# A hybrid decoder layer: state-space products in plain float32, and another order of the projection's column blocks

## The chip, the cores and the metric

The kernel runs on one NeuronCore of a Trainium2 chip. Times are microseconds on the device for one execution of the whole program; the times shown are of separate runs, the profile of one more. PE is the matrix engine (TensorE) and PEld its weight loads, DVE the VectorE, ACT the ScalarE, POOL the GpSimd, and SP the SyncE, whose queue issues all the DMAs of this kernel.

## The reference

One inference step of one decoder layer, for a prompt of 1024 tokens and 8 x 4 sampled tokens, model width 1024, everything in float32:

```
proj = rmsnorm(h) @ w_in                    # 1024 x 3072: x_ssm | z_ssm | q | k | v | z_attn, 512 each
# state-space branch: 32 groups of 16 channels, each with one 64-dim complex diagonal state
bu   = u @ Bb                               # complex
x_t  = lam * x_{t-1} + bu_t                 # scan over time
y    = Re(C x) + D u
y    = glu(gelu(y)) * silu(z_ssm)
# attention branch: 8 heads of 64; softmax over keys at three (window, dilation) patterns,
#   (128,1), (512,4), (2048,16); times silu(z_attn); the sampled tokens also look into a key and value cache
out  = rmsnorm(h + concat(rmsnorm(y_ssm), rmsnorm(y_attn)) @ w_out)
```

The prompt's keys and values, the sampled tokens' new rows and the final states are outputs too.

## The kernel before

**Numbers in two parts.** PE takes two kinds of four-byte operands here: `float32` and a rounded form, `float32r`. Nearly all products of the kernel keep precision by hand: `split` (lines 137 to 143) makes of a tile a rounded part hi (ACT copies it into a `float32r` tile, line 139) and the rest lo (DVE subtracts hi from the tile, line 140), and a product becomes three `float32r` products, hi*hi, hi*lo and lo*hi, summed in PSUM. A few products work on `float32` tiles as they are: the taps (line 622), the column sums (lines 859, 861, 1605), the products with cached values (1361, 1373), and the transposes against the identity.

**Stages.** First the inputs are normalised, transposed and split. Then the projection runs by 12 blocks of 256 columns of `w_in`: `FIRST_BLOCKS` (8 and 0), the seven of `SSM_BLOCKS`, then 6, 10 and 11 in a later stage. A block's weights come in two DMAs and are split (`win`, lines 142 and 143; 12 buffers, 8 to a block). Blocks 0 to 7, 10 and 11 come out with columns on partitions, 144 products of 352 tokens each (line 314), into two PSUM banks (`mm`) in turn; what empties a bank depends on the block: for q and k (4 to 7) a split into `eq` tiles (lines 378, 379), for z_ssm (2, 3) a tanh and a product into `stp` (lines 341 to 344), for x_ssm (0, 1) a copy. Blocks 8 and 9, the values, come out with tokens on partitions, 192 products of 256 columns (line 294), emptied by a copy on ACT (line 305), and 16 more for the sampled rows (line 410).

**The state-space stage.** Beside these blocks, `ssm(o)` works on the 32 channel groups, four at a time (o = 0 to 7). 8 tokens make one step of the scan, so that a group has 128 steps and 8 sampled rows, W = 136 columns (144 with the rows of the sampled tokens' states). A call loads `u` from DRAM, builds on POOL and DVE the matrix that takes 8 x 16 inputs to a state (`wa`, transposed on PE), the one that takes a state to 8 x 16 outputs (`f`) and rotations `rc`, `rs`, makes the direct taps (line 622) and spreads them by 8 small DMAs over a block matrix `tpl`. Then PE makes the state's input (line 658), DVE rotates it and scans it (line 669), POOL and DVE rotate it back (675 to 678) into `xx`, and `outputs` sums on PE the state's part and the taps' part (line 692), goes through a GELU on ACT (`yo`, line 694) and is stored to DRAM. `u`, the transposed matrix, `f`, `tpl` and `xx` are all split, five splits a call.

The program hands the framework `ssm(0)`, and then for each block of `SSM_BLOCKS` in turn `ssm(o + 1)`, `in_proj(blk)` and the outputs of call o (lines 697 to 705); the framework then fixes a single order for each engine. Every engine works through its own order, and a waiting instruction holds all behind it on that engine.

**After it.** From line 739 on a planner of the kernel's own (`Plan`) writes the order of the other stages: the gated linear unit (line 823), the sampled tokens' attention (991 and on), blocks 6, 10 and 11 (line 1036), the prompt's attention and the output projection.

Of the kernel before, what the change touches and what calls it, by code (L numbers as in the profile page):

```python
# [10 lines left out]
F32 = mybir.dt.float32  # L11
F32R = mybir.dt.float32r
# [9 lines left out]
DB, DS = 8, 4  # L22
# [5 lines left out]
W = NC + DB  # L28
# [75 lines left out]
def hymba_kernel(ctx: ExitStack, tc: tile.TileContext, I, O):  # L104
# [451 lines left out]

    tmp_stack.close()
    sw = pa.enter_context(tc.tile_pool(reuse_waits="tile", name="sw", bufs=1))
    tpl = sw.tile([128, 4, 128], F32, name="tpl")
    GP.memset(tpl, 0.0)  # L560

    GO = 4

    def ssm(o):
# [1 line left out]
        gs = slice(g0, g0 + GO)  # L566

        def wk(shape, name, dt=F32, bufs=1):
            if name in ("wa", "wb", "f2", "f2b", "q0", "q1", "tap", "u"):
                return sw.tile(shape, dt, tag="gen", name=name, bufs=4)  # L570
            if name in ("zz", "zb", "zs", "xx"):
                return sw.tile(shape, dt, tag="gen2", name=name, bufs=4)
            if name in ("uhl", "rc", "rs", "fhl", "thl", "xhl"):
                bufs = 2
            return sw.tile(shape, dt, tag=name, name=name, bufs=bufs)


        u = wk([128, GO, W + DB], "u")
        SY.dma_start(u, d_u[o // 2, 64 * (o % 2):64 * (o % 2) + 64].rearrange("(g c) s k -> (c s) g k", c=CH))
        uhl = wk([128, GO, 2, W + DB], "uhl", F32R)  # L580
        uh, ul = uhl[:, :, 0], uhl[:, :, 1]
        split(uh, ul, u)


        sh = [128, GO, CH, 8]
# [10 lines left out]
        GP.tensor_tensor(out=f1o, in0=pw(pr, 0, 8), in1=bc(bb, 8), op=OP.mult)  # L596
        GP.tensor_tensor(out=f1bo, in0=pw(spi, 0, 8), in1=bc(bbw, 8), op=OP.mult)
        V.tensor_tensor(out=f1, in0=f1, in1=f1b, op=OP.add)
        wh, wl = wk([128, GO, 128], "wh", F32R), wk([128, GO, 128], "wl", F32R)
        p = tp_ps([128, GO, 128])  # L600
        for g in range(GO):
            T.transpose(p[:, g, :], f1[:, g].rearrange("p c s -> p (c s)"), ident)
        split(wh, wl, p)


        sh9 = [128, GO, 9, CH]
# [1 line left out]
        GP.tensor_tensor(out=f2, in0=pw(pr, 0, 9), in1=bc(cst, 9), op=OP.mult)  # L608
        GP.tensor_tensor(out=f2b, in0=pw(pi, 0, 9), in1=bc(csw, 9), op=OP.mult)
        V.tensor_tensor(out=f2, in0=f2, in1=f2b, op=OP.add)  # L610
        fhl = wk([128, GO, 2, 128], "fhl", F32R)
        fh, fl = fhl[:, :, 0], fhl[:, :, 1]

        split(fh, fl, f2[:, :, 1:9, :].rearrange("p g t c -> p g (t c)"))


        di = wk([16, GO, 16], "di")
        GP.tensor_tensor(out=di, in0=ident[:16, :16].unsqueeze(1).to_broadcast([16, GO, 16]),
# [5 lines left out]
        for g in range(GO):  # L624
            S.activation(tap[:, g], p[32 * g:32 * g + 16], AF.Copy)
        GP.tensor_tensor(out=tap[:, :, 0:16], in0=tap[:, :, 0:16], in1=di, op=OP.add)
        for s in range(8):
            SY.dma_start(tpl[s::8, :, 16 * s:], tap[:, :, 0:128 - 16 * s])
        thl = wk([128, GO, 2, 128], "thl", F32R)
        th, tl = thl[:, :, 0], thl[:, :, 1]  # L630
        split(th, tl, tpl)


        shr = [128, GO, 8, 16]
# [19 lines left out]
        for n in (2, 2):  # L654
            p = ss_ps([128, 2, W + DB])
            for u in range(n):
                for k, (a, b) in enumerate(((wh, uh), (wh, ul), (wl, uh))):
                    T.matmul(p[:, u, :], a[:, g + u, :], b[:, g + u, :], start=(k == 0), stop=(k == 2))
            r = slice(g, g + n)
            V.tensor_tensor(out=zz[:, r], in0=p[:, :n, 0:128], in1=rc[:, r], op=OP.mult)  # L660
            V.tensor_tensor(out=zb[0:64, r], in0=p[64:128, :n, 0:128], in1=rs_[64:128, r], op=OP.mult)
            V.tensor_tensor(out=zb[64:128, r], in0=p[0:64, :n, 0:128], in1=rs_[0:64, r], op=OP.mult)
            V.tensor_tensor(out=nst[:, g0 + g:g0 + g + n, :], in0=p[:, :n, W:],
                            in1=nst[:, g0 + g:g0 + g + n, :], op=OP.add)
            g += n
# [1193 lines left out]
```

## Time and profile before

| | us |
|---|---|
| median of 3 runs (720.48 to 725.81) | 722.18 |
| the profiled execution, its own time | 725.31 |
| its span, first to last instruction | 723.5 |
| PE busy | 662.9 (92%) |
| DVE busy | 515.7 (71%) |
| ACT busy | 335.7 (46%) |
| POOL busy | 304.9 (42%) |

The profiled execution took 3.1 us more than the median, and 1.8 us of it lie outside the span. Busy shares are means over stages that have different limits, and a pipelined PE shows as busy for longer than it streams. The blocks and the state-space stage lie between 46 and 301 us of the span. One call of a matrix product can be one record in the trace (`float32r`, and the transposes) or two (`float32`: the 32 products of line 622 have 64 records, the 48 of line 1361 have 96).

### The profile page before, as it was taken

The page shows a single profiled execution, that of the slowest core. Times are in us where ns is not written, and L with a number is a line of the kernel's source. Part 1 is how long each engine was busy: PE and PEld are TensorE (multiplying, and loading weights), DVE is VectorE, ACT ScalarE, POOL GpSimd, SP SyncE. Part 2 cuts the span into 40 slices and gives each one's busy share as a digit, 9 for nine tenths or more (in the row PEclk, how much of TensorE's full clock was granted, in tenths as well). Part 3 has the DMA queues.
Part 4 walks back from the last instruction along what each step waited for, and adds up shares of the span by engine and source line. Part 5 has one row for each costly group of instructions (what it writes and reads, how often), then busy time and mean ns, then how long its engine had stood idle before and what let it go on. Part 6 is the DMA issues. An engine that isn't in the chain of part 4 may idle for free.

```text
span 723.5 us, 12491 instructions
## 1 busy us (share of the span) xinstructions
PE 662.9 (92%) x4218; PEld 603.6 (83%) x4218; DVE 515.7 (71%) x1187; ACT 335.7 (46%) x777; POOL 304.9 (42%) x291
## 2 busy tenths in 40 slices
PE   7999978888999989969899789899999699999995
PEld 5999968878999989969889788777576598888995
DVE  5997889887877875144665787468766788974486
ACT  6664253333253452253333343166566577852263
POOL 2326587764855434003575750043333446520033
PEclk9999998999999999989999899999999889999999
DMA  8612414332435542297767746288999553126123
GB/s 280 215 59 82 137 37 137 105 110 67 115 91 171 161 140 79 59 332 230 237 192 220 228 134 210 81 259 265 307 295 288 175 164 118 44 75 232 52 95 145
DMA packets 79056, 116.23 MB, mean 161 GB/s; under 512 B 15856, under 2 KB 45424, under 8 KB 78992
## 3 DMA queue, kind: packets, MB, share of 16 engines
q1 hardware_dynamic: 78992, 115.44, 50.8%
q8 instruction: 33, 0.54, 0.3%
q14 instruction: 31, 0.25, 0.1%
HBM read 83.60 MB, written 30.62 MB: 158 GB/s over the span
## 4 chain that ended last, share of the span: by engine, by line
PE 34%; DMA 13%; DVE 7%; POOL 3%; issue 3%; SPq 2%; ACT 2%; DVEq 0%; POOLq 0%; ACTq 0%
PE fo L1645 5%; DMA ct<-in_cache_v_dram 5%; PE ops L1550 4%; PE tp L294 3%; PE ss L294 3%; PE mm L294 3%; POOL dm L991 3%; PE ss L1493 3%; DMA ct<-in_cache_k_dram 3%; PE tp L1535 3%; PE mm L1036 3%; PE mm L314 2%; DMA z<-d_y 1%; PE fo L1361 1%; DMA dq<-d_pd 1%
## 5 line engine op out<-in xcount | busy, mean ns | idle before, releaser
L314 PE MATMUL mm<-xT,win 128*128 128x352 f32 x1008 | 176.2, 330 | 11.4 <-DVE eq L379 5.0
L314 PEld LDWEIGHTS mm<-xT,win 128*128 128x128 f32 x1008 | 164.3, 192 | 16.0 <-DVE eq L379 6.4
L1036 PE MATMUL mm<-xT,win 128*128 128x352 f32 x432 | 79.5, 340 | 2.5 <-DVE win L1018 2.5
L991 POOL TENSOR_TENSOR dm<-ct,dq 128x512 f32<-128x512 f32 x40 | 51.9, 1322 | 69.7 <-DMA ct<-in_cache_k_dram 47.1
L1516 POOL TENSOR_SCALAR pm<-pm,rd 128x128 f32<-128x128 f32 (+3 forms) x64 | 48.6, 762 | 76.1 <-DVE rd L1512 57.2
L1036 PEld LDWEIGHTS mm<-xT,win 128*128 128x128 f32 x432 | 73.0, 198 | 3.4 <-DVE win L1018 3.2
L1508 ACT ACTIVATE pm<-pm,mn 128x128 f32<-128x128 f32 (+3 forms) x64 | 49.5, 774 | 20.6 <-DVE mn L1496 18.5
L1542 DVE TENSOR_TENSOR pl<-tp,ph 128x512 fp32r<-128x512 f32 (+1 forms) x80 | 50.2, 632 | 5.6 <-ACT ph L1539 5.2
L1539 ACT ACTIVATE ph<-tp 128x512 fp32r<-128x512 f32 (+1 forms) x80 | 43.1, 546 | 23.3 <-PE tp L1535 17.3
L1645 PE MATMUL fo<-wo,gh 128*128 128x512 f32 x192 | 53.8, 425 | 0.0
L294 PE MATMUL mm<-win,xT 128*128 128x256 f32 x384 | 50.6, 286 | 0.1
L823 PE MATMUL gl<-yh,wg 128*128 128x272 f32 (+1 forms) x256 | 50.1, 295 | 0.0
L1496 DVE CUSTOM_DVE_ANT_0 pm<-ss,maskp 128x512 f32<-128x512 f32 (+2 forms) x64 | 37.1, 582 | 17.4 <-PE ss L1493 17.0
L294 PEld LDWEIGHTS mm<-win,xT 128*128 128x128 f32 x384 | 47.0, 190 | 0.5 <-ACT xT L139 0.4
L1535 PE MATMUL tp<-ident,pm 128*128 128x128 f32 x288 | 45.8, 278 | 0.1
L1645 PEld LDWEIGHTS fo<-wo,gh 128*128 128x128 f32 x192 | 37.2, 203 | 7.5 <-DVE mn L1496 0.2
L143 DVE SCALAR_TENSOR_TENSOR win<-wst,gin,win 128x256 fp32r<-128x256 f32 x72 | 38.7, 571 | 5.8 <-ACT win L142 5.6
L994 DVE TENSOR_REDUCE scd<-dm 128x8 f32<-128x512 f32 x40 | 27.1, 682 | 21.8 <-POOL dm L991 21.6
L823 PEld LDWEIGHTS gl<-yh,wg 128*128 128x128 f32 x256 | 41.8, 197 | 0.0
L1535 PEld LDWEIGHTS tp<-ident,pm 128*128 128x128 f32 x288 | 34.7, 142 | 7.5 <-issue 2.3
L1493 PE MATMUL ss<-ka,qt 128*128 128x512 f32 (+2 forms) x96 | 36.5, 381 | 2.4 <-DMA ka<-d_k 2.4
L823 PE MATMUL gl<-yl,wg 128*128 128x272 f32 (+1 forms) x128 | 37.2, 291 | 0.0
(402 smaller groups left out, 1475.6 us busy)
## 6 DMA issues: line engine op xcount, KB each, us to landing
wst<-in_w_in_dram SPq DMA_DIRECT2D x24, 512.0 KB
ct<-in_cache_k_dram SPq DMA_DIRECT2D x48, 256.0 KB
ct<-in_cache_v_dram SPq DMA_DIRECT2D x48, 256.0 KB
xt<-in_x_prompt_dram SPq DMA_DIRECT2D x8, 512.0 KB
wst<-in_w_out_dram SPq DMA_DIRECT2D x8, 512.0 KB
xres<-in_x_prompt_dram SPq DMA_DIRECT2D x8, 512.0 KB
qt<-d_q SPq DMA_DIRECT2D x32, 128.0 KB
qw<-d_q SPq DMA_DIRECT2D x32, 128.0 KB
```

What stands on the lines that cost most here:

```text
L294: T.matmul(out, lhs(a, kt), w(b, kt)[:, c0:c0 + cn], start=(n == 0), stop=(n == 3 * ktn - 1))
L314: T.matmul(p, w(b, kt)[:, c * 128:c * 128 + 128], x(a, kt), start=(n == 0), stop=(n == 23))
L823: T.matmul(p, wg[:, b, kt, c:c + 128], o.y[a][:, kt, :, :o.w], start=(n == 0), stop=(n == 11))
L991: GP.tensor_tensor(out=y.m, in0=y.c, in1=x.q, op=OP.mult)
L1036: T.matmul(x.p, o.w[kt][:, b, c * 128:c * 128 + 128], xT[a][:, kt, 352 * k:352 * k + 352], start=(kt == 0 and j == 0), stop=(kt == 7 and j ...
L1493: T.matmul(x.p[c][:, :w], q[:, i % 4 * 128:i % 4 * 128 + 128], o.ka[:, 512 * c:512 * c + w], start=(m == 0), stop=(m == 1))
L1508: S.activation(x.pm[:, :n], x.pm[:, :n], AF.Exp, scale=-1.0, bias=x.mn[:, nch - 1:nch], accum_out=x.dn)
L1516: a = op(PO, 0.02 + n * 0.0012, lambda: GP.tensor_scalar(x.pm[:, :n], x.pm[:, :n], x.rd, 1.0, op0=OP.mult, op1=OP.mult), pr, [a], give=["rd"])
L1535: T.transpose(x.p[:, n * 128:n * 128 + 128], o.rows[2 * m + u].pm[:, j * 128:j * 128 + 128], ident)
L1539: S.activation(x.h[:, :w], x.p[:, :w], AF.Copy)
L1542: V.tensor_tensor(out=x.l[:, :w], in0=x.p[:, :w], in1=f(x.h[:, :w]), op=OP.subtract)
L1645: T.matmul(o.f[hf], o.g[u][:, i, k], wo[0][:, j, 2 * u + k, hf * 512:hf * 512 + 512], start=(u + k + n == 0), stop=(u + k + n == 4))
```

## The change

The splits of the state-space stage go. `u` (now `chunk`), the transposed matrix (now `wt`, one copy on ACT out of PSUM), `f2`, `tpl` and `xx` are used as `float32` tiles: the state's input is one product for each group instead of three, and an output is two instead of six. `tpl` gets a second buffer, `u` three of its own, `f2` and `xx` two each; the rings of shared buffers that remain serve fewer tiles. The list of blocks has 9, a block of values, second instead of last, so that block 4, half of q, now ends the stage. Line numbers after the touched places are 7 to 13 lower.

```diff
-SSM_BLOCKS = (1, 5, 2, 3, 7, 4, 9)
+SSM_BLOCKS = (1, 9, 5, 2, 3, 7, 4)
...
-    tpl = sw.tile([128, 4, 128], F32, name="tpl")
-    GP.memset(tpl, 0.0)
+    tpls = [sw.tile([128, 4, 128], F32, name=f"tpl{i}") for i in range(2)]
+    for t in tpls:
+        GP.memset(t, 0.0)
...
-            if name in ("wa", "wb", "f2", "f2b", "q0", "q1", "tap", "u"):
+            if name in ("wa", "wb", "f2b", "q0", "q1", "tap"):
                 return sw.tile(shape, dt, tag="gen", name=name, bufs=4)
-            if name in ("zz", "zb", "zs", "xx"):
+            if name in ("zz", "zb", "zs"):
                 return sw.tile(shape, dt, tag="gen2", name=name, bufs=4)
-            if name in ("uhl", "rc", "rs", "fhl", "thl", "xhl"):
-                bufs = 2
+            if name in ("u", "rc", "rs", "f2", "xx", "wt"):
+                bufs = 3 if name == "u" else 2
...
-        u = wk([128, GO, W + DB], "u")
-        SY.dma_start(u, d_u[...])
-        uhl = wk([128, GO, 2, W + DB], "uhl", F32R)
-        uh, ul = uhl[:, :, 0], uhl[:, :, 1]
-        split(uh, ul, u)
+        chunk = wk([128, GO, W + DB], "u")
+        SY.dma_start(chunk, d_u[...])
...
-        split(wh, wl, p)
+        S.activation(wt, p, AF.Copy)
...
-        split(fh, fl, f2[:, :, 1:9, :].rearrange("p g t c -> p g (t c)"))
...
-        split(th, tl, tpl)
...
-                for k, (a, b) in enumerate(((wh, uh), (wh, ul), (wl, uh))):
-                    T.matmul(p[:, u, :], a[:, g + u, :], b[:, g + u, :], start=(k == 0), stop=(k == 2))
+                T.matmul(p[:, u, :], wt[:, g + u, :], chunk[:, g + u, :], start=True, stop=True)
...
-        split(xh, xl, xx)
...
-            for n, (a, b) in enumerate(((fh, xh), (fh, xl), (fl, xh), (th, uh), (th, ul), (tl, uh))):
-                T.matmul(p, a[:, g], b[:, g, :W], start=(n == 0), stop=(n == 5))
+            T.matmul(p, f2[:, g, 1:9, :].rearrange("p t c -> p (t c)"), xx[:, g, :], start=True, stop=False)
+            T.matmul(p, tpl[:, g], chunk[:, g, :W], start=False, stop=True)
```

The framework's order changes with it on every engine within the stage. On DVE, around the scan of the first call, before (`f` and `xx` are the tiles named above, `thl`, `fhl`, `wl`, `xhl` the lo parts, `rc` the rotation of the next call):

```order
L669 SCALAR_TENSOR_TENSOR zs<-mags,zz 128x128 x4
L610 TENSOR_TENSOR f_1170<-f_1170,f2b 128x576
L140 TENSOR_TENSOR thl<-tpl,thl 128x4x128
L140 TENSOR_TENSOR fhl<-f_1170,fhl 128x4x128
L140 TENSOR_TENSOR wl<-tp,wh 128x512
L338 COPY stp<-mm 128x4x8
L678 SCALAR_TENSOR_TENSOR xx<-zz,sg,xx 128x4x128
L140 TENSOR_TENSOR xhl<-xx,xhl 128x4x136
L645 TENSOR_TENSOR rc<-rc,q_1204 128x512
L660 TENSOR_TENSOR zz<-ss,rc 128x256
```

and with the change:

```order
L608 TENSOR_TENSOR f_1145<-f_1145,f2b 128x576
L659 SCALAR_TENSOR_TENSOR zs<-mags,zz 128x128 x4
L666 SCALAR_TENSOR_TENSOR xx<-zz,sg,xx 128x4x128
L636 TENSOR_TENSOR rc<-rc,q_1173 128x512
L650 TENSOR_TENSOR zz<-ss,rc 128x256 x2
L338 COPY stp<-mm 128x4x8
```

The four subtractions between the scan and the next call's first product are gone, and `xx` stands right behind the scan that POOL works on for it.

On PE, the end of the stage before (`so` holds an output; line 1036 is the next stage's first):

```order
L294 MATMUL mm<-win,xT_98 128x256
L410 MATMUL mm<-win,xT_97 64x256 x16
L692 MATMUL so<-xhl,fhl 128x136 x3
L692 MATMUL so<-uhl,thl 128x136 x3
L692 MATMUL so<-xhl,fhl 128x136 x3
L692 MATMUL so<-uhl,thl 128x136 x3
```

and with the change:

```order
L314 MATMUL mm<-xT_98,win 128x352
L405 MATMUL tp<-ident,pdT 32x128
L678 MATMUL so<-xx,f_3103 128x136
L679 MATMUL so<-u,tpl_1048 128x136
L678 MATMUL so<-xx,f_3103 128x136
L679 MATMUL so<-u,tpl_1048 128x136
L678 MATMUL so<-xx,f_3103 128x136
L679 MATMUL so<-u,tpl_1048 128x136
L1023 MATMUL mm<-xT_97,win 128x352 x2
```

The last outputs now follow block 4's columns; three of the last four groups come there, where all four came before. From line 1036 (now 1023) on the order of PE is the same row for row, and so are the other engines' orders from there on.

## Rows read from the trace of the kernel before

**Rows 1.** Busy by stretch: length; PE, PEld, DVE, ACT, POOL busy; PE clock; DMA.
```profile
46.00:301.00 255.00, 238.18 (x1627) 230.40 (x1625) 196.65 (x330) 100.66 (x260) 140.34 (x120) 0.98 0.35 107
100.00:140.00 40.00, 35.87 (x222) 34.24 (x221) 37.53 (x54) 15.72 (x40) 30.21 (x26) 0.91 0.33 106
109.40:116.20 6.80, 6.80 (x30) 6.80 (x29) 6.80 (x13) 2.90 (x7) 3.69 (x3) 0.50 0.57 185
```
**Rows 2.** Groups of PE, 46 to 301 us: busy, mean ns, then idle before and releasers.
```profile
L314 PE MATMUL mm<-xT,win 128*128 128x352 f32 x1008 | 176.2, 330 | 11.4 <-DVE eq L379 5.0 <-DVE stp L344 2.6 <-DVE win L143 2.0
...
L658 PE MATMUL ss<-uhl,wl 128*128 128x144 f32 x32 | 8.4, 277 | 1.7 <-DVE wl L140 1.5
L602 PE MATMUL tp<-ident,wa 128*128 128x128 f32 x32 | 5.5, 298 | 0.9 <-DVE wa L598 0.9
L622 PE MATMUL ss<-f,bb 128*16 128x128 f32 x64 | 3.3, 278 | 2.8 <-DVE f L610 2.8
```
**Rows 3.** PE in order of time: start, length, instructions merged by line and tiles.
```profile
74.74 0.66 PE L602 MATMUL tp<-ident,wa 128*128 128x128 f32 x4
75.15 1.85 PE L314 MATMUL mm<-xT,win 128*128 128x352 f32 x10
76.94 0.41 PE L622 MATMUL ss<-f,bb 128*16 128x128 f32 x8
77.28 1.71 PE L314 MATMUL mm<-xT,win 128*128 128x352 f32 x9
...
103.11 0.45 PE L692 MATMUL so<-xhl,fhl 128*128 128x136 f32 x3
...
104.40 1.83 PE L314 MATMUL mm<-xT,win 128*128 128x352 f32 x10
...
276.91 19.70 PE L294 MATMUL mm<-win,xT 128*128 128x256 f32 x164
296.45 1.98 PE L410 MATMUL mm<-win,xT 128*64 128x256 f32 x16
298.27 0.45 PE L692 MATMUL so<-xhl,fhl 128*128 128x136 f32 x3
```
**Rows 4.** The subtractions of line 140, all tiles, 46 to 301 us: DVE busy.
```profile
46.00:301.00 255.00, 43.24 (x40) 0.98 0.35 107
```
**Rows 5.** Groups of DVE, 46 to 301 us: busy, mean ns, then idle before.
```profile
L140 DVE TENSOR_TENSOR uhl<-u,uhl 128x576 fp32r<-128x576 f32 x8 | 13.0, 1622 | 2.5 <-ACT uhl L139 2.5
...
L140 DVE TENSOR_TENSOR xhl<-xx,xhl 128x544 fp32r<-128x544 f32 x8 | 8.2, 1028 | 7.2 <-ACT xhl L139 7.2
...
L140 DVE TENSOR_TENSOR wl<-tp,wh 128x512 fp32r<-128x512 f32 x8 | 5.4, 680 | 0.2 <-ACT wh L139 0.2
...
L678 DVE SCALAR_TENSOR_TENSOR xx<-zz,sg,xx 128x512 f32<-128x512 f32 x8 | 13.7, 1714 | 13.2 <-POOL zz L677 13.2
```
**Rows 6.** PE around products of float32, and a run of 272 columns, as in rows 3.
```profile
330.05 0.41 PE L823 MATMUL gl<-yh,wg 128*128 128x272 f32 x2
...
331.56 1.14 PE L1036 MATMUL mm<-xT,win 128*128 128x352 f32 x6
...
358.11 0.61 PE L859 MATMUL so<-ones,acc 128*128 128x1 f32 x4 [0.96 <-POOL acc L846]
358.57 0.37 PE L861 MATMUL so<-acc,all 128*128 128x16 f32 x2
358.80 0.50 PE L823 MATMUL gl<-yh,wg 128*128 128x272 f32 x2
...
561.63 1.05 PE L1373 MATMUL kt<-dm,selb 128*32 128x512 f32 x2
562.61 0.33 PE L1493 MATMUL ss<-ka,qt 128*128 128x128 f32 x1
```
**Rows 7.** PE at the start of the next stage, as in rows 3.
```profile
301.00 16.59 PE L1036 MATMUL mm<-xT,win 128*128 128x352 f32 x102
...
323.64 0.40 PE L1098 MATMUL tp<-ident,pdT 128*32 128x128 f32 x1 [5.94 <-ACT pdT L1047]
```

More of the change, by code (lines that the diff above doesn't have):

```diff
@@ L568, in wk @@
         def wk(shape, name, dt=F32, bufs=1):
-            if name in ("wa", "wb", "f2", "f2b", "q0", "q1", "tap", "u"):
+            if name in ("wa", "wb", "f2b", "q0", "q1", "tap"):
                 return sw.tile(shape, dt, tag="gen", name=name, bufs=4)
-            if name in ("zz", "zb", "zs", "xx"):
+            if name in ("zz", "zb", "zs"):
                 return sw.tile(shape, dt, tag="gen2", name=name, bufs=4)
-            if name in ("uhl", "rc", "rs", "fhl", "thl", "xhl"):
-                bufs = 2
+            if name in ("u", "rc", "rs", "f2", "xx", "wt"):
+                bufs = 3 if name == "u" else 2
             return sw.tile(shape, dt, tag=name, name=name, bufs=bufs)
-        u = wk([128, GO, W + DB], "u")
-        SY.dma_start(u, d_u[o // 2, 64 * (o % 2):64 * (o % 2) + 64].rearrange("(g c) s k -> (c s) g k", c=CH))
-        uhl = wk([128, GO, 2, W + DB], "uhl", F32R)
-        uh, ul = uhl[:, :, 0], uhl[:, :, 1]
-        split(uh, ul, u)
+        chunk = wk([128, GO, W + DB], "u")
+        SY.dma_start(chunk, d_u[o // 2, 64 * (o % 2):64 * (o % 2) + 64].rearrange("(g c) s k -> (c s) g k", c=CH))
         sh = [128, GO, CH, 8]
@@ L598, in ssm @@
         V.tensor_tensor(out=f1, in0=f1, in1=f1b, op=OP.add)
-        wh, wl = wk([128, GO, 128], "wh", F32R), wk([128, GO, 128], "wl", F32R)
+        wt = wk([128, GO, 128], "wt")
         p = tp_ps([128, GO, 128])
@@ L610, in ssm @@
         V.tensor_tensor(out=f2, in0=f2, in1=f2b, op=OP.add)
-        fhl = wk([128, GO, 2, 128], "fhl", F32R)
-        fh, fl = fhl[:, :, 0], fhl[:, :, 1]
-        split(fh, fl, f2[:, :, 1:9, :].rearrange("p g t c -> p g (t c)"))
         di = wk([16, GO, 16], "di")
@@ L626, in ssm @@
         GP.tensor_tensor(out=tap[:, :, 0:16], in0=tap[:, :, 0:16], in1=di, op=OP.add)
+        tpl = tpls[o % 2]
         for s in range(8):
             SY.dma_start(tpl[s::8, :, 16 * s:], tap[:, :, 0:128 - 16 * s])
-        thl = wk([128, GO, 2, 128], "thl", F32R)
-        th, tl = thl[:, :, 0], thl[:, :, 1]
-        split(th, tl, tpl)
         shr = [128, GO, 8, 16]
@@ L672, in ssm @@
         x1 = xx[:, :, 1:NC + 1]
-        xhl = wk([128, GO, 2, W], "xhl", F32R)
-        xh, xl = xhl[:, :, 0], xhl[:, :, 1]
         GP.tensor_tensor(out=x1, in0=zs, in1=rc, op=OP.mult)
@@ L681, in ssm, with outputs @@
         S.activation(xx[:, :, NC:], x0[:, gs, :], AF.Copy)
-        split(xh, xl, xx)
-        return lambda: outputs(o, fh, fl, xh, xl, th, tl, uh, ul)
-    def outputs(o, fh, fl, xh, xl, th, tl, uh, ul):
+        return lambda: outputs(o, f2, xx, tpl, chunk)
+    def outputs(o, f2, xx, tpl, chunk):
         g0 = GO * o
```

## The prediction

> **What bounds the kernel now.** I read the busy times by stretch first, then PE's groups in the stretch that the change touches, then PE in order of time for the pace of each kind of product. From 46 to 301 us, the blocks and the state-space stage, PE is busy for 238 of 255 us; DVE for 197, in the worst 40 us for 37.5 [rows 1]. So PE bounds the stage and DVE is close behind: of the waits in front of PE's groups, 16.8 us in all (11.4 + 1.7 + 0.9 + 2.8), every releaser that is named is a DVE line [rows 2]. The reader should see there that PE never waits for the state-space chain's end, but for what DVE does late: emptied banks (`eq`, `stp`), split weights, the matrices of the next call.
>
> How much of the 255 us is work at PE's steady pace? A product of 352 columns takes 0.163 us (102 in 16.59 us [rows 7]), one of 256 takes 0.119 (164 between 276.91 and 296.45), one of the sampled rows 0.114 (16 in 1.82), four transposes 0.41, the taps of a call 0.34, and the twelve short `float32r` products between 103.11 and 104.40 us 0.1075 each [rows 3]. The stage has 1008 of the first (164.3 us), 192 of the second in block 9 (22.8), 32 of the third (3.6), 8 times four transposes (3.3), 8 times the taps (2.7), and 96 + 192 = 288 state-space products (31.0). That makes 227.7 us; the other **27.3 us** are the waits, the restarts behind them and the clock: from 109.4 to 116.2 us it is granted at half, 1.2 GHz instead of 2.4, and 30 products start there where 42 would at 0.163 us, 1.9 us lost [rows 1]. PE had waited on DVE's `win` just before.
>
> **The change, part by part.**
>
> *Products on PE.* A call of four groups had 12 + 24 `float32r` products and gets 4 + 8 `float32` ones, 96 over the stage. A `float32` product has two records, each with a weight load. No row shows one of 136 columns on all 128 rows and columns of the array. Nearest rows: with 512 columns, two records take 0.98 us (561.63 to 562.61), 0.49 each, while 512 columns passed twice at 2.4 GHz are 0.43; so a record passes its columns twice, and 136 cost what 272 do, 0.126 us (twelve between 330.05 and 331.56). With hardly any columns (1 and 16) records come every 0.115 us, the pace of the weight loads [rows 6]. Ends: 0.115 us below; above, 0.49 scaled to 136 columns, 0.130, and to 144, 0.138. I take 0.126 for the 128 records of 136 columns and 0.133 for the 64 of 144, since the run of 272 columns is nearest in shape: 16.1 + 8.5 = 24.6 us for 31.0 before, **6.4 us less** (5.5 to 8.9 by the ends). It lies on PE's path whole.
>
> What the pages make of it: the Trainium skill ("FP8 and Floating Point Precision", TensorE Precision Notes) says that true float32 goes through the array in four passes; the trace agrees as to the passes, two records of two each. By its count alone, four passes for three, the products would take a third more, and the change would lose 10.3 us on PE. The rows say otherwise because a short `float32r` product doesn't pay for its columns: 136 are 0.057 us at 2.4 GHz, and it takes 0.1075 [rows 3]; it pays for a weight load, of which a product now needs two instead of three.
>
> *Splits.* All 40 subtractions of line 140 in the stage go, 43.2 us of DVE [rows 4], far more than 40 times the 0.68 us that the one from PSUM takes: those from SBUF average up to 1.62 us [rows 5], beside POOL's work. With them go DVE's waits for ACT's halves, 7.2 us at `xhl` and 2.5 at `uhl`. ACT loses four of five copies a call. DVE's load falls from 197 to 153 us of a stage of some 232, two thirds instead of 77%. None of it is a gain in itself; what counts is how much of the 27.3 us it takes along. One wait goes with its cause (`wl`, 1.5 us). The others are DVE arriving late, and DVE keeps one cause of it: it stands at `xx` for POOL's rotation, 13.2 us in the stage [rows 5], longer than at the two splits named above (9.7). In the new order `xx` is still behind a scan, with banks to empty behind it. So I take 60%, **16.4 us**, between ends of nothing and all.
>
> *Order of blocks.* Block 9 has 24.6 us of PE work that ask little of DVE (no bank of it is split), block 4 has 23.5 us that ask for six subtractions. Moving 9 to second place puts light work where DVE was fullest, and leaves DVE busier at the end, where before it had slack. Its cover there is the relief just counted. On SP's queue block 4's last stores stand ahead of the last outputs' stores and of the loads of `z`; the values' stores stood there before. PE issues 6 products of output at the end for 24, which shortens the tail by 2.6 - 0.8 us (part of the 6.4). The next stage has 102 products ready to cover the turnover, 16.6 us, and then waits 5.9 us for the same chain of loads as before [rows 7]. I count nothing, plus or minus 3 us in the range.
>
> *Buffers.* `tpl` and `u` no longer wait for a split but for PE's last product on them; with two and three buffers a call has the next call's time to spare. `q` and `tap` follow a shorter ring of shared buffers whose users are now POOL's and DVE's own steps. Nothing counted.
>
> *Sum.* 6.4 + 16.4 = 22.8 us. Everything behind the stage keeps its order on all engines and shifts as it is. Against the profiled execution's 725.3 us that makes 702.5; the median stands 3.1 us lower, so **about 700 us** (699.4).
>
> **The rivals.** One per cent, what can be told from no change here, is 7.2 us: 715.0 to 729.4.
>
> 1. *POOL sets the pace.* POOL's steps aren't fewer, and DVE, sooner at `xx`, only waits there longer, with full banks behind it; the stalls stay and only the products count: 722.2 - 6.4 = 716. For it: the 13.2 us at `xx`. Against: POOL is busy for 140 of 255 us [rows 1], and most of PE's waits name other DVE lines.
> 2. *All stalls go*, and the clock stays at full: 722.2 - 6.4 - 27.3 = 688.5. For it: every named wait is DVE's. Against: 13.2 us at `xx` remain.
> 3. *Four passes, four loads*: each `float32` product costs as much as four short ones now, 96 x 0.43 = 41.3 us, 10.3 more than now; less 16.4, 716. Against: two records a product, not four. It is how the page's count would show.
> 4. *Slower: a float32 weight load can't run ahead.* If each record waited for the array to empty and then loaded, it would pay the load, 0.115 us, and a hand-over of the size seen in front of the taps (ten products of 352 in 1.79 us between 75.15 and 76.94 for 1.63, so 0.16 [rows 3]): 0.275 x 192 = 52.8 us on top. 722.2 - 22.8 + 52.8 = 752. It decides from 22.8 / 192 = 0.12 us a record. For it: the taps, the `float32` products that stand beside block products today, do cost that. Against: the taps load 16 columns on strips of the array, and the full-width `float32` records at 358.11 us follow each other, and are followed by `float32r` ones, at 0.115 us with nothing between [rows 6].
> 5. *The change doesn't take.* The order on DVE and PE shows that it does.
>
> **How the numbers follow.** Forecast 0.70, POOL's pace 0.13, all stalls 0.08, four loads 0.04, no load ahead 0.05. The forecast's own range is 692 to 711 (gain of 40 to 85% of the stalls, products at either end, the turnover's 3 us). The range goes on to 688 and 716, which takes in most of the cases at its ends and leaves out the slow one: about 8 in 10. Faster by over 1%: the forecast, all stalls, and a few of the cases at 716, 0.82. Within 1%: most of the cases at 716, 0.12. Slower: 0.06.
>
> **What would show it.** State products at about 0.133 us a record and outputs at 0.126 (0.5 us for a group's four); if they stand 0.25 or more apart, case 4. DVE busy for some 150 us in the stage; PE's waits on it 4 to 10 us instead of 16.8, with fewer stretches at 1.2 GHz. The first product of the next stage (line 1023) at about 278 us instead of 301; from there on the same distances to the end. I am wrong if PE's waits stay above 12 us (then look for `xx` behind POOL), if the stage's gain is given back in the turnover, or if a `float32` record isn't near 0.13 us.

## The result, and the profile after

The changed kernel takes **703.9 us** (median of 4 runs, 700.5 to 704.9) against 722.6 before: a ratio of 0.973, 95% interval 0.970 to 0.976, so 18.7 us less. A second series of the same kernel (e11 below) gave 0.970 (0.966 to 0.974). The forecast was 700, range 688 to 716. The total came out; two of its terms did not, and they erred in opposite directions, so the nearness of the total is in part luck.

Read first the busy times of the stage that the change touches, then of the two stretches in it where PE's clock is at half (start, length, PE, PEld, DVE, ACT, POOL busy, PE clock, DMA share, GB/s; of the changed kernel):

```profile
46.00:284.80 238.80, 226.44 (x1533) 220.85 (x1531) 166.17 (x290) 83.05 (x229) 128.96 (x119) 0.98 0.37 113
75.70:79.10 3.40, 3.40 (x13) 3.40 (x13) 3.40 (x4) 0.49 (x2) 3.37 (x4) 0.50 0.01 2
120.10:126.90 6.80, 6.15 (x33) 5.74 (x34) 4.16 (x7) 2.13 (x8) 4.39 (x5) 0.50 0.67 186
```

The stage is 16.5 us shorter (46.22 to 301.00 us before, 46.46 to 284.79 now, from the first block product to the first of line 1023). DVE has 40 instructions fewer, but its busy time fell by 30.5 us [rows 1], not by the 43.2 that the subtractions had taken [rows 4]: what stays on DVE got slower. PE runs at 1.2 GHz for 10.2 us of the stage, as long as before (6.8 us [rows 1] and another 3.4 at 174 us).

PE's groups that wait, 46 to 284.8 us (busy, mean ns, then idle before and releasers):

```profile
L314 PE MATMUL mm<-xT,win 128*128 128x352 f32 x1008 | 172.9, 328 | 3.7 <-DVE eq L379 1.3 <-DVE stp L338 1.3 <-DVE stp L342 1.2
L294 PE MATMUL mm<-win,xT 128*128 128x256 f32 x198 | 27.5, 299 | 1.5 <-DVE win L143 1.5
...
L600 PE MATMUL tp<-ident,wa 128*128 128x128 f32 x32 | 5.0, 274 | 1.9 <-DVE wa L596 1.9
L615 PE MATMUL ss<-f,bb 128*16 128x128 f32 x64 | 3.5, 294 | 5.2 <-DVE f L608 5.2
```

The sum is 12.3 us, against 16.8 [rows 2]. The wait on split weights is gone, the one on emptied banks fell from 11.4 to 3.7, and the wait on `f` rose from 2.8 to 5.2. The releasers are DVE's sums and its `win` steps, and on DVE those same lines stand out (46 to 284.8 us, busy, mean ns, idle before):

```profile
L143 DVE SCALAR_TENSOR_TENSOR win<-wst,gin,win 128x256 fp32r<-128x256 f32 x60 | 43.5, 774 | 4.1 <-ACT win L142 4.0
L608 DVE TENSOR_TENSOR f<-f,f2b 128x576 f32<-128x576 f32 x8 | 17.4, 2172 | 7.6 <-POOL xx L668 6.5 <-POOL f2b L607 1.1
...
L666 DVE SCALAR_TENSOR_TENSOR xx<-zz,sg,xx 128x512 f32<-128x512 f32 x8 | 10.9, 1360 | 16.8 <-POOL zz L665 16.8
```

The same two groups before, which the forecast had not looked at (46 to 301 us):

```profile
L143 DVE SCALAR_TENSOR_TENSOR win<-wst,gin,win 128x256 fp32r<-128x256 f32 x60 | 32.3, 571 | 4.3 <-ACT win L142 4.1
L610 DVE TENSOR_TENSOR f<-f,f2b 128x576 f32<-128x576 f32 x8 | 11.5, 1437 | 0.0
```

As many steps of the same size take 17.1 us more (11.2 for `win`, 5.9 for `f`). One `win` undisturbed is 0.47 us, one `f` 0.75.

The products themselves, at the end of the stage (PE in order of time: start, length, then instructions merged):

```profile
275.01 0.39 PE L678 MATMUL so<-xx,f 128*128 128x136 f32 x2
275.24 0.39 PE L679 MATMUL so<-u,tpl 128*128 128x136 f32 x2
275.38 7.95 PE L314 MATMUL mm<-xT,win 128*128 128x352 f32 x48
...
283.52 0.39 PE L679 MATMUL so<-u,tpl 128*128 128x136 f32 x2
283.75 0.40 PE L678 MATMUL so<-xx,f 128*128 128x136 f32 x2
283.98 0.40 PE L679 MATMUL so<-u,tpl 128*128 128x136 f32 x2
...
309.01 0.40 PE L1085 MATMUL tp<-ident,pdT 128*32 128x128 f32 x1 [7.48 <-ACT pdT L1034]
```

Two records every 0.23 us, with nothing between them: a `float32` record of 136 columns costs 0.116 us (the median over the 128 of the stage, start to next start), close to the 0.115 of the full-width records of 1 and 16 columns [rows 6], not the 0.126 of 272 columns. The 64 records of 144 columns cost 0.122 (also a median), while `float32r` products of 136 and of 144 columns both stand 0.11 apart (0.112 and 0.111 in the kernel before). So the `float32` price here does go with the columns: 8 more take 0.006 us more, and two passes of 8 columns at 2.4 GHz would be 0.0067 (an estimate). The last row is the turnover: the wait for the chain of loads grew from 5.9 [rows 7] to 7.5 us.

**An account of the stage.** For each kernel below I took from the trace the time from each product's start to the next one's, and set against each kind its median. What is above the medians is called *excess*: waits, restarts and half clock together. The rest is steady work, of which only the state-space products differ between kernels (288 x 0.112 = 32.3 us, or 128 x 0.116 + 64 x 0.122 = 22.7).

| kernel | ratio to before (95%) | stage, us | products, steady | excess | PE idle over 0.15 us | one `win`, ns | longest `f`, us |
|---|---|---|---|---|---|---|---|
| before | 1 | 254.8 | 32.3 | 29.6 | 16.6 | 571 | 1.8 |
| after | 0.973 (0.970 to 0.976) | 238.3 | 22.7 | 22.1 | 12.4 | 774 | 7.5 |
| e1: order of blocks alone | 1.000 (0.997 to 1.004) | 254.7 | 32.3 | 29.4 | 14.5 | 587 | 2.0 |
| e2: after, old order | 0.976 (0.970 to 0.983) | 237.5 | 22.7 | 21.3 | 11.1 | 796 | 7.5 |
| e3: before, no subtractions | 0.986 (0.980 to 0.992) | 243.0 | 32.3 | 17.6 | 9.1 | 647 | 2.0 |
| e4: after, splits as idle work | 0.993 (0.990 to 0.996) | 250.6 | 22.7 | 34.3 | 21.6 | 657 | 2.0 |
| e5: after, fewer POOL products | 0.962 (0.959 to 0.965) | 229.4 | 22.7 | 13.4 | 6.3 | 556 | 8.7 |
| e6: after, DVE makes all matrices | 0.966 (0.961 to 0.971) | 234.1 | 22.7 | 17.9 | 8.8 | 538 | 1.6 |
| e7: after, DVE makes the rotations | 0.972 (0.965 to 0.978) | 237.3 | 22.7 | 21.2 | 12.9 | 552 | 2.1 |
| e8: after, POOL makes two sums | 0.977 (0.974 to 0.980) | 239.9 | 22.7 | 23.7 | 14.1 | 838 | on POOL |
| e9: after, early rotations | 0.971 (0.967 to 0.975) | 234.7 | 22.7 | 18.5 | 11.2 | 772 | 3.6 |
| e10: e9 with the old order | 0.974 (0.970 to 0.978) | 236.8 | 22.7 | 20.5 | 12.3 | 833 | 2.1 |
| e11: after once more | 0.970 (0.966 to 0.974) | 237.2 | 22.7 | 21.0 | 13.5 | 772 | 7.4 |
| e12: after, DVE makes `f` | 0.979 (0.975 to 0.982) | 238.3 | 22.7 | 22.1 | 12.9 | 704 | 6.3 |

Behind the stage each profiled execution has another 413 to 422 us of span (before 422.5, after 418.3, e7 413.2), with no trend by what was changed in the stage; the stage's column is free of that scatter, the ratio has the interval.

### The profile page after: what moved, and what is told of

The parts are those of the page before. It is cut to its first block, busy times and chain, and to the rows that moved or that the text cites. A ratio compares the mean times of both kernels' runs of the same rounds, so it can differ in the third digit from the quotient of the medians.

```text
span 703.1 us, 12224 instructions
## 1 busy us (share of the span) xinstructions
PE 650.1 (92%) x4122; PEld 594.0 (84%) x4122; DVE 486.1 (69%) x1147; ACT 318.3 (45%) x745; POOL 294.1 (42%) x292
## 4 chain that ended last, share of the span: by engine, by line
PE 53%; DVE 17%; DMA 12%; POOL 7%; issue 4%; ACT 4%; SPq 2%; DVEq 0%; POOLq 0%; ACTq 0%
PE mm L314 13%; PE fo L1632 5%; PE ops L1537 4%; PE mm L294 4%; DMA ct<-in_cache_v_dram 4%; PE mm L1023 4%; PE ss L294 3%; PE tp L294 3%; PE ss L1480 3%; PE tp L1522 3%; POOL dm L978 3%; DMA ct<-in_cache_k_dram 3%; DVE win L143 3%; DVE pm L1483 1%; PE fo L1348 1%
## 5 line engine op out<-in xcount | busy, mean ns | idle before, releaser
L314 PE MATMUL mm<-xT,win 128*128 128x352 f32 x1008 | 172.9, 328 | 3.7 <-DVE eq L379 1.3
L1023 PE MATMUL mm<-xT,win 128*128 128x352 f32 x432 | 78.9, 338 | 2.8 <-DVE win L1005 2.8
L1495 ACT ACTIVATE pm<-pm,mn 128x128 f32<-128x128 f32 (+3 forms) x64 | 49.5, 773 | 20.2 <-DVE mn L1483 17.9
L294 PE MATMUL mm<-win,xT 128*128 128x256 f32 x384 | 53.5, 294 | 1.7 <-DVE win L143 1.5
L143 DVE SCALAR_TENSOR_TENSOR win<-wst,gin,win 128x256 fp32r<-128x256 f32 x72 | 50.0, 742 | 5.5 <-ACT win L142 5.4
L1526 ACT ACTIVATE ph<-tp 128x512 fp32r<-128x512 f32 (+1 forms) x80 | 43.1, 547 | 22.4 <-PE tp L1522 16.4
L1632 PE MATMUL fo<-wo,gh 128*128 128x512 f32 x192 | 51.8, 412 | 0.0
L294 PEld LDWEIGHTS mm<-win,xT 128*128 128x128 f32 x384 | 49.2, 197 | 2.6 <-DVE win L143 2.1
L1483 DVE CUSTOM_DVE_ANT_0 pm<-ss,maskp 128x512 f32<-128x512 f32 (+2 forms) x64 | 37.1, 582 | 16.5 <-PE ss L1480 16.1
L1632 PEld LDWEIGHTS fo<-wo,gh 128*128 128x128 f32 x192 | 35.5, 194 | 6.9 <-DVE mn L1483 0.2
```

The source lines that it names most:

```text
L294: T.matmul(out, lhs(a, kt), w(b, kt)[:, c0:c0 + cn], start=(n == 0), stop=(n == 3 * ktn - 1))
L314: T.matmul(p, w(b, kt)[:, c * 128:c * 128 + 128], x(a, kt), start=(n == 0), stop=(n == 23))
L1023: T.matmul(x.p, o.w[kt][:, b, c * 128:c * 128 + 128], xT[a][:, kt, 352 * k:352 * k + 352], start=(kt == 0 and j == 0), stop=(kt == 7 and j ...
L1495: S.activation(x.pm[:, :n], x.pm[:, :n], AF.Exp, scale=-1.0, bias=x.mn[:, nch - 1:nch], accum_out=x.dn)
L1632: T.matmul(o.f[hf], o.g[u][:, i, k], wo[0][:, j, 2 * u + k, hf * 512:hf * 512 + 512], start=(u + k + n == 0), stop=(u + k + n == 4))
```

## The experiments

### Taking the change apart: e1 to e4

Three things change at once: the price of the products on PE, the load on DVE, and the order of the blocks. Four kernels take them apart. A fourth thing they don't separate: with the change the framework also fixes another order on each engine, and it does so anew in every kernel. My theory by then (A) was that the products' price gave some 10 us and the relief of DVE some 7; the rivals were that the order did it (O), that the order cost (C), that DVE's load is what counts as the prediction had it, or that it doesn't count (N).

**e1, the order alone.**

```diff
-SSM_BLOCKS = (1, 5, 2, 3, 7, 4, 9)
+SSM_BLOCKS = (1, 9, 5, 2, 3, 7, 4)
```

> The kernel before with only the new list of blocks (9 second, 4 last); products and splits as before. Theory A (the gain of the change is the products' price on PE, some 10 us, and some 7 us of stalls that went with the subtractions; the order of blocks is worth little by itself): 719 to 726 us. Theory O (the order is what takes late waits away): 706 to 716. Theory C (block 9's eight win steps land where DVE is already held beside POOL): 725 to 732, PE waits on win up from 2.0 to 4 us or more.

Measured 720.6 against 720.9, ratio 1.000 (0.997 to 1.004). The order is worth nothing by itself. Theory C's sign shows, 2.4 us of PE's waits on `win` in block 9, but the waits in front of line 314 fall from 11.4 to 5.1.

**e2, everything but the order.**

```diff
-SSM_BLOCKS = (1, 9, 5, 2, 3, 7, 4)
+SSM_BLOCKS = (1, 5, 2, 3, 7, 4, 9)
```

> The changed kernel with the list of blocks of before (9 last): float32 products and no splits. Theory A: 701 to 708, the same as the change within 1%. Theory O: 710 to 720. Theory C (the new place of block 9 costs): 695 to 700, with the one step f of 7.5 us still there, but the eight win steps of block 9 short (about 0.5 us each).

702.0 us, ratio 0.976 (0.970 to 0.983): the same as the change. I had expected of theory C that the `win` steps would be short again; they take 796 ns on the mean, no better than 774, because block 5's eight `win` steps then stand in that place beside POOL (11.86 us from 107.04 on).

**e3, the subtractions alone.**

```diff
-        split(uh, ul, u)
+        S.activation(uh, u, AF.Copy)
+        ul = uh
...
```

The transposed matrix, `f`, `tpl` and `xx` are treated alike.

> The kernel before without the 40 subtractions of line 140 in the state-space stage (the rounded parts stand in for the lo parts, so every product is still three float32r products, 288 in all); the copies on ACT and the order of blocks stay. Theory A: the products' price stays, 7 us of stalls go: 712 to 718. As the prediction had it (60% of the stalls hang on DVE's load, 16.4 us): 703 to 709. Theory N (DVE's load doesn't matter, POOL's pace does): 720 to 724.

710.1 us, ratio 0.986 (0.980 to 0.992), 10.9 us less than before: between theory A (712 to 718) and the prediction's 60% (703 to 709). In the stage it is 11.8 us, all of it excess (29.6 to 17.6).

**e4, the products without the relief.**

```diff
+        uhl = wk([128, GO, 2, W + DB], "uhl", F32R)
+        split(uhl[:, :, 0], uhl[:, :, 1], chunk)
...
```

The parts of `wt`, `f2`, `tpl` and `xx` are made alike.

> The changed kernel with the five splits of each call put back as work whose results nobody reads (ACT copies and DVE subtractions); float32 products, new order of blocks. Theory A: the products' price alone, 709 to 716. As the prediction had it (products 6.4 us, stalls on DVE's load): 714 to 721. Theory N (DVE's load doesn't matter): 702 to 707.

715.8 us, ratio 0.993 (0.990 to 0.996), 5.1 us less than before: at the slow end of theory A's range and inside the prediction's (714 to 721) too, so the time does not tell these two apart. The products are 9.6 us cheaper on PE, and half of that is lost again to excess, 34.3 us for 29.6. The groups of PE tell where (46.1 to 296.7 us, busy, mean ns, idle before):

```profile
L314 PE MATMUL mm<-xT,win 128*128 128x352 f32 x1008 | 176.0, 332 | 10.4 <-DVE stp L338 5.7 <-ACT ek L384 2.5 <-DVE eq L379 1.7
...
L623 PE MATMUL ss<-f,bb 128*16 128x128 f32 x64 | 3.6, 297 | 10.0 <-DVE f L614 10.0
```

The wait for `f` in front of the taps, 2.8 us before [rows 2], is 10.0 here, which is more than the whole rise of the excess. Is it that a PE with cheaper products comes sooner to an `f` that comes no sooner? The trace says no. Nearly all of it is two waits, in the calls 0 and 2 (PE, then DVE, in order of time):

```profile
71.09 0.60 PE L604 MATMUL tp<-ident,wa 128*128 128x128 f32 x4
76.02 0.48 PE L623 MATMUL ss<-f,bb 128*16 128x128 f32 x8 [4.33 <-DVE f L614]
...
126.13 0.63 PE L623 MATMUL ss<-f,bb 128*16 128x128 f32 x8 [5.46 <-DVE f L614]
...
66.82 7.31 DVE L140 TENSOR_TENSOR uhl<-u,uhl 128x576 fp32r<-128x576 f32 x1 [1.24 <-ACT uhl L139]
74.06 1.91 DVE L614 TENSOR_TENSOR f<-f,f2b 128x576 f32<-128x576 f32 x1
...
124.15 1.92 DVE L614 TENSOR_TENSOR f<-f,f2b 128x576 f32<-128x576 f32 x1
```

In call 0 no state-space product has run yet, in either kernel, so their price can play no part. `f` is done at 75.97 us, before at 76.55; PE is there at 71.69 instead of 76.94 because its order is another. 144 products of line 314 stand ahead of the taps where 176 stood before (and in e1 and e3), 10 of them between the transposes and the taps [rows 3]; 32 products are 5.2 us at 0.163. Neither the list of blocks nor the subtractions set this number: e2, with the old list, has 144 as well, and e3, without the subtractions, 176. In call 2 the kernel to compare with is e1, which has the same list of blocks:

```profile
121.97 0.63 PE L622 MATMUL ss<-f,bb 128*16 128x128 f32 x8 [2.18 <-DVE f L610]
...
120.00 1.92 DVE L610 TENSOR_TENSOR f<-f,f2b 128x576 f32<-128x576 f32 x1
```

There PE stands before the taps from 119.80 us on, in e4 from 120.67: not sooner, and `f` comes 4.2 us later. So the wait in call 0 comes of the order on PE, and the one in call 2 of a later `f`; what delays that `f`, and what the other waits of e4 come of (5.7 us on `stp` above all), these runs don't show.

As sums the four fit together. Relief lowers the excess by 12.0 us with the old products (29.6 to 17.6) and by 12.2 with the new (34.3 to 22.1). The new products, with the buffers and the order that come with them, take 9.6 us off the steady work and add about 4.6 to the excess, with the splits (29.6 to 34.3) and without (17.6 to 22.1). 9.6 - 4.6 + 12.1 = 17.1, against 16.5 us in the stage. No kernel has the new products with the old buffers and order. So the price of the order by itself was not measured, and what in the change brings it about, the new buffers or the new products, stays open.

### Why 22 us of excess are left: e5 to e8

What holds DVE's sums and its `win` steps? Between 107 and 119 us POOL has eight products in a row (POOL in order of time: start, length; of the changed kernel):

```profile
107.10 1.65 POOL L663 TENSOR_TENSOR xx<-zs,rc 128x512 f32<-128x512 f32 x1 [1.34 <-DVE zs L659]
108.83 1.36 POOL L664 TENSOR_TENSOR zz<-zs,rs 64x512 f32<-64x512 f32 x1
110.24 1.36 POOL L665 TENSOR_TENSOR zz<-zs,rs 64x512 f32<-64x512 f32 x1
111.68 1.44 POOL L634 TENSOR_TENSOR rc<-cosk 128x512 f32<-128x512 f32 x1
113.07 1.58 POOL L637 TENSOR_TENSOR rs<-cosk,sink 128x512 f32<-128x512 f32 x1
114.61 1.41 POOL L606 TENSOR_TENSOR f<-pr,cst 128x576 f32<-128x576 f32 x1
...
116.03 1.55 POOL L635 TENSOR_TENSOR q<-sink 128x512 f32<-128x512 f32 x1
117.54 1.54 POOL L638 TENSOR_TENSOR q<-sink,cosk 128x512 f32<-128x512 f32 x1
```

and DVE in the same time, with two rows from a little earlier:

```profile
102.78 0.42 DVE L652 TENSOR_TENSOR zb<-ss,rs 64x256 f32<-64x256 f32 x1
...
103.32 2.30 DVE L656 SCALAR_TENSOR_TENSOR zz<-zb,sgn,zz 128x512 f32<-128x512 f32 x1
...
107.52 11.85 DVE L143 SCALAR_TENSOR_TENSOR win<-wst,gin,win 128x256 fp32r<-128x256 f32 x8
119.29 0.74 DVE L666 SCALAR_TENSOR_TENSOR xx<-zz,sg,xx 128x512 f32<-128x512 f32 x1
119.95 0.75 DVE L608 TENSOR_TENSOR f<-f,f2b 128x576 f32<-128x576 f32 x1
```

Eight `win` steps take 11.85 us, 1.48 each for 0.47 alone: one step to each of POOL's, as if the two took turns. `zb` at 102.78, which reads one operand from PSUM, keeps its 0.42 us though POOL works on line 637 and 595 from 101.39 to 103.96; `zz` right behind it, with both operands in SBUF, takes 2.30 for 0.74. `xx` stands 7.7 us behind block 9's steps, with POOL's part done at 111.60. And in call 0 the sum `f` stands from 67.08 to 74.55 us beside POOL's next row of products; the PE row behind it is the 2.5 us wait after which the clock fell at 75.7:

```profile
65.69 5.94 PE L314 MATMUL mm<-xT,win 128*128 128x352 f32 x36
71.47 0.60 PE L600 MATMUL tp<-ident,wa 128*128 128x128 f32 x4
74.60 0.41 PE L615 MATMUL ss<-f,bb 128*16 128x128 f32 x8 [2.54 <-DVE f L608]
74.94 5.34 PE L314 MATMUL mm<-xT,win 128*128 128x352 f32 x22
```

The Trainium skill ("SBUF — State Buffer", SBUF: two separate sides) says that VectorE and GpSimd share one pair of SBUF ports under an exclusive lock, that a VectorE instruction with two SBUF inputs contends for it with a GpSimd instruction that reads SBUF, and that the loser waits for the whole instruction. The rows above agree as to who is held and who isn't. By that rule a sum would wait for the one POOL product that runs; here one is held for five (67.25 to 73.93 us), and the measurement decides.

The theories for the next four: H, DVE is held beside POOL's products, and what is left of the excess comes of that; T, the number of DVE's steps is what counts.

**e5, POOL's load taken away.**

```diff
-        GP.tensor_tensor(out=rc, in0=ea(ear), in1=eb(ebr), op=OP.mult)
...
+        if o == 0:
+            for t, a, b in zip(four, (ear, eai, ear, eai), (ebr, ebi, ebi, ebr)):
+                GP.tensor_tensor(out=t, in0=ea(a), in1=eb(b), op=OP.mult)
-        V.tensor_tensor(out=rc, in0=rc, in1=q0, op=OP.subtract)
+        V.tensor_tensor(out=rc, in0=four[0], in1=four[1], op=OP.subtract)
```

> The changed kernel with POOL's four products for the rotations rc and rs made in call 0 alone and read by DVE's sums in all calls (the rotations of calls 1 to 7 are left out): 28 POOL steps of 1.4 to 1.9 us fewer, DVE has as many steps as before. Theory H (a DVE step with two operands from SBUF is held while POOL works, and that is what is still late): the 60 win steps fall from 774 ns to under 650, no f step over 2 us, PE's waits in the stage from 12.4 to 5 to 8 us, 694 to 700 us. Theory T (it is DVE's number of steps): 701 to 707, the win steps about as long as they are. Theory L (the loads and the blocks' own banks limit): the win steps get shorter, the time stays at 701 to 707.

696.2 us, ratio 0.962 (0.959 to 0.965). With as many DVE steps as in the changed kernel their time falls (busy in the stage, columns as above: DVE 143.6 where it was 166.2, POOL 88.2 for 129.0):

```profile
46.00:275.00 229.00, 222.74 (x1526) 218.14 (x1524) 143.59 (x290) 81.78 (x227) 88.21 (x91) 0.99 0.38 118
```

DVE in call 0, in order of time:

```profile
66.20 8.71 DVE L609 TENSOR_TENSOR f<-f,f2b 128x576 f32<-128x576 f32 x1 [1.12 <-POOL f2b L608]
74.84 3.95 DVE L143 SCALAR_TENSOR_TENSOR win<-wst,gin,win 128x256 fp32r<-128x256 f32 x5
```

Theory T is out: the same 290 DVE instructions, 9 us less of stage. (POOL's other products can come sooner too when it has fewer; e5 doesn't tell that from the hold.) H was right on the `win` steps (556 ns) and on PE's idle time (6.3 us), wrong on one point: the long `f` of call 0 is there still, 8.7 us, since call 0's four products still stand in a row on POOL (66.39 to 71.90 us), and PE waits 3.8 us for it.

**e6 and e7, POOL's products moved to DVE** (all eight of a call; only the four of the rotations).

```diff
-        GP.tensor_tensor(out=rc, in0=ea(ear), in1=eb(ebr), op=OP.mult)
+        V.tensor_tensor(out=rc, in0=ea(ear), in1=eb(ebr), op=OP.mult)
...
```

e7 moves `rc`, `q0`, `rs_` and `q1`, e6 also `f1o`, `f1bo`, `f2` and `f2b`.

> The changed kernel with all eight products a call that POOL makes for the matrices and rotations moved to DVE (64 steps; POOL keeps the rotation of the states). Theory H: POOL falls from 132 to about 45 us in the stage, DVE gains 64 steps of about 0.7 us (45 us) and loses about as much of being held (win at 774 instead of 473 ns is 18 us, the f steps 11, the others some 15), so DVE's busy time stays near 180 and the time at 695 to 705. Theory T: DVE at 225 us of the stage becomes the bound, 715 to 730.

> The changed kernel with only the four products a call for the rotations rc and rs moved from POOL to DVE (32 steps). Theory H: half of the above: POOL at about 85 us in the stage, DVE near 180, 696 to 702 us. Theory T: DVE about 200 us busy, 707 to 716.

699.8 (0.966, 0.961 to 0.971) and 703.1 (0.972, 0.965 to 0.978), the first inside H's range, the second 1 us above its own. DVE is busy for 191 and 179 us of a stage of some 236, where T would have had 225 and 200; POOL for 61 and 96, more than I had reckoned. But H's gain stayed out: in e6 `win` and `f` are short again (538 ns, 1.6 us at most), and PE waits 6.4 us on `wa` (4.17 of it at 103.8 us), which now queues behind DVE's other new work. In e7 they are short as well (552 ns, 2.1 us at most), and PE waits 10.0 us for emptied banks (5.8 of it on `stp`). So short `win` and `f` steps alone don't take the excess away. e6 is the fastest kernel here that computes everything; its interval touches the changed kernel's, so I don't call it faster.

**e8, DVE's sums moved to POOL.**

```diff
-        V.tensor_tensor(out=f1, in0=f1, in1=f1b, op=OP.add)
+        GP.tensor_tensor(out=f1, in0=f1, in1=f1b, op=OP.add)
...
```

The sum `f2` goes to POOL too.

> The changed kernel with the two sums a call that end the matrices wa and f moved from DVE to POOL (16 steps of 1.2 to 1.5 us there; DVE loses 24 us of busy time, 11 of it one of being held). Theory H: the f step of 7.5 us and PE's wait of 2.5 us behind it go, but POOL works 20 us more and holds the win steps longer (800 to 900 ns): 699 to 706. Theory T (fewer steps on DVE is all that counts): 692 to 698.

707.0 us, 0.977 (0.974 to 0.980), 1 us past H's range and far from T's: DVE has 16 steps fewer, and PE now waits 8.3 us for `win` (838 ns each) and 3.2 for POOL's own sums.

### Can the hold be moved away? e9 to e12

POOL idles from 41.5 to 61 us, since the buffers of its first products lie where the constants' scratch memory was. e9 gives the rotations their own memory, so that four products run there instead of beside `f`.

```diff
     sp = pa.enter_context(tc.tile_pool(reuse_waits="tile", name="sp", bufs=1))
+    sr = pa.enter_context(tc.tile_pool(reuse_waits="tile", name="sr", bufs=1))
     tmp_stack = ExitStack()
...
-            return sw.tile(shape, dt, tag=name, name=name, bufs=bufs)
+            return (sr if name in ("rc", "rs") else sw).tile(shape, dt, tag=name, name=name, bufs=bufs)
```

> The changed kernel with the buffers of rc and rs in a pool opened ahead of the constants' scratch memory, so that POOL's four products for the rotations of calls 0 and 1 needn't wait for that scratch and go into POOL's idle time from about 49 to 61 us instead of standing behind f2b at 67 to 74 us. Theory H: the f step of 7.5 us falls below 2.5, PE's wait of 2.5 us before the taps of call 0 and the half clock behind it go, 697 to 702 us. Theory W (the hold only moves: POOL at 49 to 55 us holds DVE's chain that makes bb, and wa comes 3 us later): 702 to 707, PE waiting on wa or win near 75 us instead.

> The same early rotations with the list of blocks of before (9 last). Theory H: 696 to 701, level with the one above within 0.5%. Theory W: 701 to 706.

> The changed kernel once more, on the same chip as the two above, to compare with: 701 to 706 us by every theory, with the f step of 7.5 us again.

701.6 and 703.7 us, with 701.6 for the changed kernel on the same chip: nothing gained. Both theories were half right. The `f` of call 0 fell to 3.6 us and PE's wait for it went, 2.5 us; and DVE's chain that makes the constants is held instead (DVE in e9, in order of time; its `ex_q` steps take 0.2 us when POOL is idle):

```profile
48.59 1.32 DVE L438 TENSOR_TENSOR ex_q<-ex_q,ex_r 128x64 f32<-128x64 f32 x1
49.94 1.32 DVE L439 TENSOR_SCALAR ex_q<-ex_q 128x64 f32<-128x64 f32 x1
51.18 1.66 DVE L143 SCALAR_TENSOR_TENSOR win<-wst,gin,win 128x256 fp32r<-128x256 f32 x1
```

PE then waits at 52.9, 54.6 and 59.6 us, 3.6 us in all, and the clock falls at 59.5 us. In e11, the changed kernel again, PE waits 2.5 us until 74.1 as well, yet the clock stays at 2.4 GHz until 120.4; so the fall at 75.7 in the first profile was not the rule. The stage is 2.5 us shorter than in e11; the medians don't show it.

**e12, only `f` on DVE.**

```diff
-        GP.tensor_tensor(out=f2, in0=pw(pr, 0, 9), in1=bc(cst, 9), op=OP.mult)
+        V.tensor_tensor(out=f2, in0=pw(pr, 0, 9), in1=bc(cst, 9), op=OP.mult)
...
```

So is the product `f2b`.

> The changed kernel with only the two products a call for the matrix f moved from POOL to DVE (16 steps of about 0.75 us there, 16 of 1.2 to 1.7 us fewer on POOL), so that f's sum waits for nothing of POOL's and POOL's run of products from 62 us on is 2.9 us shorter. Theory H: PE's waits on f (5.2 us in the stage) fall below 2.5, POOL at about 110 us in the stage, 696 to 701. Theory W (the hold only moves, here to the sum wa, which stands behind f's steps on DVE): waits on wa grow from 1.9 to 4 us or more, 701 to 706.

705.4 us, 0.979 (0.975 to 0.982): theory W. The sum `f`, though both its products are DVE's own now, is held for 6.3 us from 65.42 on beside POOL's four rotation products (65.50 to 71.09), and `wa` stands behind it: PE waits 7.5 us on `wa` in the stage.

## Why the prediction came out right, step by step

**What bounds the stage:** right. PE bounds it with DVE close behind, and every wait of PE's that matters is for something late on DVE. e3 shows it by itself: nothing but DVE's subtractions left out, 10.9 us gained.

**Products on PE, 6.4 us:** the mechanism was right (two records, and for each the time of two passes, as the 0.006 us for 8 columns bears out), the size off. Measured 9.6 us: 0.116 and 0.122 us a record instead of 0.126 and 0.133, and 0.112 for a short `float32r` product instead of 0.1075. I took the run of 272 columns because it was nearest in shape, but those are `float32r` products; two passes of 136 columns take less time than one of 272. The lower end of the range, 0.115 from the full-width records of 1 and 16 columns [rows 6], was close for 136 columns and 6% too low for 144; it would have given 8.9 us.

**Splits and stalls, 16.4 us:** this step failed. The excess fell by 7.5 us (29.6 to 22.1), a quarter, not 60%, below the 40% at the low end of my range for it. A part is the size of the relief: left out alone, the subtractions take 12.0 us with them (e3), 41%. The other part is, in call 0 at least, a term that I had put at nothing. "Buffers: nothing counted" and the paragraph on the order looked at the blocks and the tail, not at where the framework would put the taps and `f`. The new products come with about 4.6 us more of excess, and in e4 the waits for `f` are more than that. In the changed kernel call 0's taps, too, stand behind 144 products instead of 176, and PE waits 2.5 us there; with the 32 it would have come 5.2 us later, after `f` (an estimate from these counts and times). How much of the 4.6 is the order's beyond call 0 stays open.

**What is late next:** named, but the wrong place of it. I expected DVE to stand at `xx` for POOL's rotation, and it does, 16.8 us for 13.2 [rows 5]; PE never waits for that. What PE waits for is the DVE steps that POOL's products slow: `f` and `wa`, and `win`. The prediction had the row for it, subtractions of 0.68 us from PSUM and up to 1.62 on the mean from SBUF, "beside POOL's work", and used it only to price what goes, not what stays: the remaining `win` and `f` steps took 17.1 us more than before, which is why DVE's busy time is 166 and not the 150 that I named. The test I set, PE's waits above 12 us, was met at 12.3, and it pointed at POOL, rightly in the engine and wrongly in the tile.

**Order of blocks, nothing:** right (e1, and e2 against the change). **Buffers, nothing:** not tried alone; PE's named waits are for none, but the framework's new order comes with them or with the new products, and that is not nothing (above). **Turnover, no more than 3 us:** 1.5 us more wait than before, and 3.4 us more at half clock.

**The rivals.** POOL's pace (716) was wrong as a time, but its engine does keep part of the excess in place: with 28 of its products left out, 8.7 of the 22.1 us go (e5). All stalls go: out. Four passes, four loads: out by the spacing, 0.23 us for a product where it needed 0.43. By the Trainium skill's count ("FP8 and Floating Point Precision", TensorE Precision Notes) of four passes the products would have lost time; the trace's products gained 9.6 us. No load ahead (752): out, records follow each other and the block products with no gap. The first product of the next stage came at 284.8 us, not 278, and the shorter rest made up for some of it.

So the total is 4 us off by three errors: the products 3.2 us better than said, the stalls 8.9 us worse, and some 2 us in which single executions differ behind the stage. The first and the last hide more than half of the second, which is luck.

## What to carry to other kernels

A change of tiles and buffers can let the framework fix another order on every engine. Before you put that at nothing, look in the new order for what stands ahead of each product that waits: here 32 block products fewer stood ahead of the first taps, and PE came to them 5 us sooner than before. Where a change touches two engines, a kernel for each part alone (e3 and e4) gives each part's share, but only for the order that each of these kernels gets. And price a short matrix product by what its own kind of record costs: the `float32r` ones cost the same at 136 and 144 columns (0.11 us), the `float32` ones 0.116 and 0.122.

## What the runs showed of the hardware

- A `float32` product of 136 columns is two records 0.116 us apart, one of 144 columns two records 0.122 apart; three `float32r` products of either shape take 3 x 0.112 us. In plain `float32` these short full-width products are 31% and 27% cheaper, not dearer.
- A DVE step that reads two operands from SBUF takes as long as POOL's product beside it (`win` 1.48 us for 0.47), steps with an operand in PSUM keep their time (0.42), and in e9 a step with a single SBUF operand, line 439, was held too (1.32 us for 0.20).
- A DVE sum can be held through a whole row of POOL products: 7.5, 8.7 and 6.3 us for 0.75. Its end falls in each case where POOL stops for a moment (two memsets at 73.88 us in the changed kernel; POOL itself waiting for `f` in e5 and e12). In e4 a subtraction of the same size was held for 7.3 us in the same place. The `win` steps got a turn after every product. What makes the difference between the two stays open; I didn't try a sum of another size or place in memory there.
- Work moved between DVE and POOL, in either direction (e6, e7, e8, e12), left the time within 1% of the changed kernel's, with intervals that touch or overlap; only POOL work left out (e5) gave about 1%, clear of its interval.
